# Attention values as seven block products, interleaved with the first query and key tiles

## The chip, the cores and the metric

The kernel runs on one core of one Trainium2 chip. The metric is the device time of one execution in microseconds. The core has a matrix engine (PE), a vector engine (DVE), an activation engine (ACT), a general engine (POOL), and SP, which here only issues DMAs. Each engine executes its own list of instructions in the order in which the program lists them; an instruction waits until the semaphores it names have reached a count, and everything behind it on the same engine waits with it.

## The reference, cut to what matters

Two layers on 512 tokens of 1024 features. Layer 0 mixes tokens with a gated linear recurrence, layer 1 with stick-breaking attention of 16 heads; after each mixer comes a SwiGLU feed-forward block (FFN), and every sub-layer is preceded by an RMS norm. The change touches layer 1 between its input and its first heads:

```
h   = rmsnorm(x, g)                       # 512 x 1024
qkv = h @ w_qkv                           # q, k, v: 512 x 1024 each, 16 heads of 64
z   = q k^T / 8;  w = exp(log_sigmoid(z) + suffix sums of log_sigmoid(-z)), masked
o   = w v                                 # per head
```

The sum `h @ w_v` is what is computed differently: a 512x1024 by 1024x1024 product.

## The kernel before, in words

Activations are kept transposed: `x[k]` holds features 128k to 128k+127 of all 512 tokens, 128 x 512. Everything is float32, and each product of two float32 numbers is made from three passes of the matrix engine: each factor is split into a high part (rounded to a shorter format, names ending in h) and a low part (the remainder, ending in l), and high times high, high times low and low times high are added in an accumulator bank (`bank`, eight of them, 128 x 512 each). So a weight chunk of 128 x 1024 goes through one DMA into a buffer (`raw`, `bu` or `bv`), one cast on ACT (`wh`) and one subtraction (`wl`) on DVE or POOL. `wh` and `wl` have three buffers each. The list `chunks` fixes in which order weight chunks are loaded, split and used; `chunk()` takes the next one and issues the splits and loads that lie a set number of chunks ahead.

The FFNs already use seven block products instead of eight: tokens are halved, features are halved, sums of quarters of the activations are formed on DVE and split by ACT and DVE, sums of quarters of the weights are formed by DMAs that add into their destination (`Piece.plus`, issued on POOL's queue), and the halves of the outputs are added up afterwards. `Piece` and `Unit` describe this.

In layer 1 the order around the change is this. At the end of the first FFN the last products are added to `x` (`take(m)`, DVE), and `gain(m)` makes the operands `uh` (ACT, x times the norm's gain) and `ul` (DVE) and the squares for the norm (ACT, summed in `acc` by POOL; the last one by DVE). `back(h)` transposes the FFN's output on PE. Between `back(0)` and `back(1)` stands the first of the value chunks. After it come, for two halves of the value columns, the products of all eight k with the four token tiles, 24 matmuls per chunk, eight chunks; between them the norm's statistics (`norm_rs1`: four small matmuls, a square root on ACT and a Newton step on DVE; `norm_rs2`: four transposing matmuls and a copy). The two halves are scaled and split into `vs` (ACT and DVE, `L1124` and `L1125`). Then come the query and key tiles (`proj(t)`, 24 matmuls, in two parts of 12; even t are queries, odd t keys), the first scores (`s1(0)`), the chain on them (`chain_a(0)`: nine activations on ACT, six DVE instructions, three on POOL), and `rsum`. From there a loop over heads takes scores, suffix sums (`s2`) and weighted values (`s3`) in turn, one more `proj` tile beside each head.

In the FFNs and from the first `proj` on, PE, ACT, DVE and POOL run in the order in which the code issues instructions. Between them, in the setup of the attention stage and in the value products, a scheduler orders them.

Of the kernel before, what the change touches and what calls it, by code (L numbers as in the profile page):

```python
# [10 lines left out]
F32 = mybir.dt.float32  # L11
F32R = mybir.dt.float32r
# [158 lines left out]
class Kern:  # L171
# [155 lines left out]
    def chunk(self, ahead=None):  # L327
# [9 lines left out]
        more = 11 if ffn else self.AHEAD_LOAD  # L337
# [201 lines left out]

        return gather, half, root, chain, store  # L540

    def v_chunk(self, pv, c):
        wh, wl = self.chunk()
        for kk in range(2):
            k = 2 * c + kk
            cs = ts(kk, S)
            for t in range(NT):
                uh, ul = self.u[k]
                self.mm3(pv[t], uh[:, ts(t)], ul[:, ts(t)], wh[:, cs], wl[:, cs], k == 0, k == KT - 1)

    def rglru(self):
        nc, tc = self.nc, self.tc
# [182 lines left out]
    def ffn(self, l, gnext):  # L735
# [3 lines left out]
        with tc.tile_pool(name=f"ffn{l}", bufs=1) as self.fp, \  # L739
# [2 lines left out]
            self.ffn_end = self.after[l] or len(self.chunks)  # L742
            self.hold = len(self.chunks)
            for i in range(self.used + 1, len(self.chunks)):
                if isinstance(self.chunks[i], Piece) and not isinstance(self.chunks[i - 1], Piece):
# [258 lines left out]
            if gnext:  # L1004
# [68 lines left out]
    def attention(self):  # L1073
# [5 lines left out]
        with ExitStack() as cx:  # L1079
# [28 lines left out]
                self.mi += 1  # L1108
                return mb[self.mi % len(mb)]

            for half in range(2):
                pv = [self.bank[4 - 4 * half + t] for t in range(NT)]
                for c in range(1 - half, 4):
                    self.v_chunk(pv, c)
                if half == 0:
                    self.bi = 2
                    self.norm_rs1()
                for t in range(NT):
                    r = self.rsT[:, t:t + 1]
                    pvv = pv[t].rearrange("p (h d) -> p h d", d=64)  # L1120
                    for j in range(2):
                        v = vs[t][2 * half + j] = self.new("vs", F32R, shape=[P, 4, P])
                        pj = pvv[:, 4 * j:4 * j + 4, :]
                        nc.scalar.activation(v[:, :, 0:64], pj, AF.Copy, scale=r)  # L1124
                        nc.vector.scalar_tensor_tensor(v[:, :, 64:128], pj, r, v[:, :, 0:64].bitcast(F32),  # L1125
                                                       ALU.mult, ALU.subtract)
                if half == 0:
                    self.bi = 3
                    self.norm_rs2()
            tc.keep_in_program_order(nc.scalar.preload_act_table_set("natural_log_exp_and_others"))  # L1130

            heads = {}
            self.qrel = []

            def proj(t, part):
                if part == 0:
                    self.pt = mps()
# [142 lines left out]
            E = mybir.EngineType  # L1280
            with tc.manual_schedule(engines={E.PE, E.Activation, E.DVE, E.Pool}):
                self.wl_dve = True
                for t in range(3):
                    proj(t, 0)
                    if t == 2:
                        s1(0)
                        chain_a(0)
                        for i in range(3):
                            rsum(0, i)
                    proj(t, 1)  # L1290
                    proj_evac1(t)
                    proj_evac2(t)
                self.wl_dve = False
                def osplit(p):
                    oh, ol = ou[p] = self.new("oh", F32R, True), self.new("ol", F32R, True)
# [116 lines left out]
def layout(inp):  # L1412
# [18 lines left out]
    v = wv.reshape(4, 2, P, 2, S).transpose(3, 0, 2, 1, 4).reshape(8, P, 1024)  # L1431
# [48 lines left out]
```

## Time and profile before

| | |
|---|---|
| median of 3 runs | 1103.15 us (1102.72 to 1103.34) |
| the profiled execution's own time | 1102.71 us |
| span of its trace | 1101.0 us |
| mean granted clock of PE | 0.998 |
| PE busy | 1087.4 us, 99% |
| DVE, ACT, POOL busy | 896.4, 710.8, 363.5 us |
| DMA | 159.87 MB, mean 145 GB/s |

The trace counts microseconds from the span's start. A row of its timeline gives start, duration, engine, line and operation with the tiles that it writes and reads. The duration of a matmul includes the passage through the array; consecutive matmuls overlap, and their rate is read from the distance of their starts. The value products run from 492.4 to about 539.8, the first query tiles from there, the first scores at 553.43, those of the second head at 560.42.

### The profile page before, as it was taken

To read this page: it belongs to the slowest core of one execution; us is meant where nothing else is said; L and a number is where in the kernel's file an instruction comes from. 1 tells how busy PE (TensorE), PEld (TensorE's weight loads), DVE (VectorE), ACT (ScalarE), POOL (GpSimd) and SP (SyncE) were. 2 spreads that over 40 slices of the span, in tenths; PEclk is the share of its full clock that TensorE was granted. 3 is DMA by queue.
4 is the path that set the end of the run, shared out by engine and by line. 5 is a ranking of instruction groups with operands and counts; after the bars stand their busy time and mean duration, and the time that the engine had idled before them with its cause. 6 is when DMAs were issued, how large, how long until landed. Compare 5 with 4: busy or idle time off the path is not lost.

```text
span 1101.0 us, 14735 instructions
## 1 busy us (share of the span) xinstructions
PE 1087.4 (99%) x5255; PEld 907.8 (82%) x5255; DVE 896.4 (81%) x1250; ACT 710.8 (65%) x1084; POOL 363.5 (33%) x273
## 2 busy tenths in 40 slices
PE   9999999999999999999999999999999999999996
PEld 6888888888888888888888888788888888888885
DVE  6967787687978888986378889978578797978897
ACT  6697667565546464635379999967764555546454
POOL 1652332324151413204034445413132424151412
PEclk9999999999999999999999999999999999999999
DMA  8532339877677776443243433234986777765522
GB/s 298 147 97 91 115 113 217 193 215 163 163 192 155 202 166 174 90 140 96 76 116 100 127 80 96 60 100 135 216 179 207 157 198 164 163 194 119 149 67 76
DMA packets 47385, 159.87 MB, mean 145 GB/s; under 512 B 5712, under 2 KB 5968, under 8 KB 47312
## 3 DMA queue, kind: packets, MB, share of 16 engines
q1 hardware_dynamic: 34640, 113.32, 31.8%
q0 software_dynamic: 12384, 45.09, 23.5%
q8 instruction: 41, 0.67, 0.3%
q10 hardware_dynamic: 288, 0.52, 0.1%
q14 instruction: 32, 0.26, 0.1%
HBM read 148.43 MB, written 2.10 MB: 137 GB/s over the span
## 4 chain that ended last, share of the span: by engine, by line
PE 75%; DVE 9%; ACT 4%; issue 3%; DVEq 0%
PE bank L771 17%; PE bank L772 17%; PE bank L773 17%; PE bank L350 6%; PE bank L352 6%; PE bank L351 6%; DVE wl L315 3%; PE bank L1238 2%; DVE y L763 1%; PE bank L778 1%; PE bank L1264 1%; ACT t L1202 1%; ACT t L1201 1%; ACT wh L313 1%; DVE ks L1167 1%
## 5 line engine op out<-in xcount | busy, mean ns | idle before, releaser
L315 DVE TENSOR_TENSOR wl<-raw,wh 128x1024 fp32r<-128x1024 f32 x114 | 171.6, 1507 | 39.9 <-ACT wh L313 39.5
L313 ACT CAST wh<-raw 128x1024 fp32r<-128x1024 f32 x134 | 140.1, 1048 | 94.9 <-PE bank L773 37.2
L771 PE MATMUL bank<-wh,ow 128*128 128x512 f32 (+1 forms) x480 | 179.6, 374 | 0.5 <-DVE b L763 0.5
L773 PE MATMUL bank<-wh,ow 128*128 128x512 f32 (+1 forms) x480 | 178.3, 372 | 0.0
L772 PE MATMUL bank<-wl,ow 128*128 128x512 f32 (+1 forms) x480 | 178.3, 371 | 0.0
L92 POOL DMA_DIRECT2D bu<-w_gu x64 | 56.1, 877 | 277.3 <-DMA bu<-w_gu 159.1
L313 ACT CAST wh<-bu 128x1024 fp32r<-128x1024 f32 x66 | 69.5, 1053 | 65.1 <-PE bank L773 39.8
L315 DVE TENSOR_TENSOR wl<-bu,wh 128x1024 fp32r<-128x1024 f32 x66 | 82.9, 1273 | 28.9 <-ACT wh L313 28.1
L771 PEld LDWEIGHTS bank<-wh,ow 128*128 128x128 f32 x480 | 90.4, 188 | 16.7 <-issue 1.3
L773 PEld LDWEIGHTS bank<-wh,ow 128*128 128x128 f32 x480 | 90.4, 188 | 15.7
L772 PEld LDWEIGHTS bank<-wl,ow 128*128 128x128 f32 x480 | 90.5, 188 | 15.4
L350 PE MATMUL bank<-uh,wh 128*128 128x512 f32 x256 | 101.5, 398 | 1.4 <-ACT wh L656 1.4
L351 PE MATMUL bank<-ul,wh 128*128 128x512 f32 x256 | 99.6, 390 | 0.0
L352 PE MATMUL bank<-uh,wl 128*128 128x512 f32 x256 | 99.5, 391 | 0.0
L763 DVE TENSOR_TENSOR y<-y,bank 128x512 f32<-128x512 f32 x140 | 89.0, 679 | 2.2 <-PE bank L773 2.1
L315 POOL TENSOR_TENSOR wl<-raw,wh 128x1024 fp32r<-128x1024 f32 x22 | 55.8, 2540 | 80.1 <-ACT wh L313 68.4
L771 PE MATMUL bank<-wh,hth 128*128 128x512 f32 (+1 forms) x194 | 75.4, 389 | 0.0
L772 PE MATMUL bank<-wl,hth 128*128 128x512 f32 (+1 forms) x194 | 75.3, 388 | 0.0
L773 PE MATMUL bank<-wh,htl 128*128 128x512 f32 (+1 forms) x194 | 75.1, 387 | 0.0
L315 DVE TENSOR_TENSOR wl<-bv,wh 128x1024 fp32r<-128x1024 f32 x44 | 58.3, 1337 | 13.3 <-ACT wh L313 13.2
L1206 POOL TENSOR_TENSOR spl<-t,sph 128x512 fp32r<-128x512 f32 (+1 forms) x32 | 38.9, 1235 | 82.9 <-DVE sph L1205 80.7
L350 PEld LDWEIGHTS bank<-uh,wh 128*128 128x128 f32 x256 | 48.0, 188 | 11.5 <-ACT wh L656 2.5
(277 smaller groups left out, 2770.3 us busy)
## 6 DMA issues: line engine op xcount, KB each, us to landing
bu<-w_gu POOLq DMA_DIRECT2D x64, 512.0 KB, 5.8
raw<-w_gu SPq DMA_DIRECT2D x44, 512.0 KB, 4.1
raw<-w_dn SPq DMA_DIRECT2D x24, 512.0 KB, 5.4
bu<-w_gu SPq DMA_DIRECT2D x22, 512.0 KB, 4.3
bv<-w_gu SPq DMA_DIRECT2D x22, 512.0 KB, 4.1
bv<-w_gu POOLq DMA_DIRECT2D x22, 512.0 KB, 6.4
d<-w_dn SPq DMA_DIRECT2D x20, 512.0 KB, 3.7
raw<-w_qk SPq DMA_DIRECT2D x16, 512.0 KB, 3.6
```

Source lines behind the costliest of these rows:

```text
L92: kern.soon(lambda: kern.nc.gpsimd.dma_start(t, self.part(n), accum_op=ALU.add))
L313: (self.nc.vector.tensor_copy if self.wh_dve else self.nc.scalar.copy)(wh[:, c], raw)
L315: self.wli = self.wl_engine(i).tensor_tensor(wl[:, c], raw, wh[:, c].bitcast(F32), ALU.subtract)
L350: mm(out, lhsT=wh, rhs=xh, start=first, stop=False)
L351: mm(out, lhsT=wh, rhs=xl, start=False, stop=False)
L352: mm(out, lhsT=wl, rhs=xh, start=False, stop=last)
L763: add = lambda o, a, b: nc.vector.tensor_tensor(o, a, b, ALU.add)
L771: mm(out, lhsT=xh, rhs=wh, start=first, stop=False, skip_group_check=True)
L772: mm(out, lhsT=xh, rhs=wl, start=False, stop=False, skip_group_check=True)
L773: mm(out, lhsT=xl, rhs=wh, start=False, stop=last, skip_group_check=True)
L1206: nc.gpsimd.tensor_tensor(sl[:, w], sp[:, w], sh[:, w].bitcast(F32), ALU.subtract)
L1238: mm(zt[kt][:, o0:o0 + ZW[j]], lhsT=tri if j == kt else one_n, rhs=s_, start=False, stop=True, skip_group_check=True)
```

## The change

The value product is cut into two halves of tokens (columns 0 to 255 and 256 to 511 of the transposed activations, `lo` and `hi`), two halves of features (k 0 to 3 and 4 to 7) and two halves of value columns. It is made from seven block products instead of eight, numbered 1 to 7. Each has two weight chunks of 12 matmuls. `VUnit` gives them, and the three query and key chunks between them, their order: product 1, query/key tiles 0, 1, 2, products 5, 3, 6, 2, 7, 4. Eight accumulating DMAs of 512 KB, two to a sum, make the weight sums in the buffers `bu` and `bv`: `bu` gets a second quarter for product 5, a third for 6 and a fourth for 4; `bv` gets a second quarter for 7. Those for product 5 are issued ahead of the stage. The prefetch of the second FFN's first chunks into the same two buffers moves behind the value products.

The activation sums are formed in two steps for each k of 0 to 3: `vops1(k)` makes two scaled copies of x (ACT), a difference and a second difference of 128 x 256 (DVE), and splits the result (`vh` by ACT, `vl` by DVE); `vops2(k)` makes two more sums of 128 x 256 and splits them. Products 5 and 6 need `vops1`, 3 and 7 need `vops2`; 1, 2 and 4 use the plain `uh` and `ul`.

Three bank pairs are used: A (4, 5), B (2, 3) and B2 (0, 1). Product 1 is written to A and copied to `r1`; 5 to B and copied to `b5`; 3 is added on top of B, 6 on top of A; A is copied to `u2`, to which B is added; 2 goes to B2 and is added to `r1`; 7 on top of A, added to `b5`; 4 on top of A. Each finished half is scaled and split into `vs` (`v_evac`). `norm_rs1`, `norm_rs2` and `vops2` stand around product 5, the evacuations of tiles 0 to 2 around product 3. `s1(0)`, `chain_a(0)` and `rsum` now stand ahead of product 4, and the third query/key tile is no longer split around them. The loop over heads is unchanged.

On ACT, from the norm's table load on. `vs` are the values, `acc` receives the norm's broadcast, `wh` are weight casts. Before:

```order
L469 ACT_TABLE_LOAD
L469 ACTIVATE x_79<-bank_72,eps 128x4
L1124 ACTIVATE vs_4349<-bank_74,x_79 128x4x64
L1124 ACTIVATE vs_4355<-bank_75,x_79 128x4x64
L1124 ACTIVATE vs_4361<-bank_76,x_79 128x4x64
L1124 ACTIVATE vs_4367<-bank_77,x_79 128x4x64
L1124 ACTIVATE vs_4352<-bank_74,x_79 128x4x64
L1124 ACTIVATE vs_4358<-bank_75,x_79 128x4x64
L491 COPY acc<-bank_73 128x512
L1124 ACTIVATE vs_4364<-bank_76,x_79 128x4x64
L1124 ACTIVATE vs_4370<-bank_77,x_79 128x4x64
L313 CAST wh_4434<-raw_4013 128x1024
```

And now, where `vh` are the activation sums, `vb` the copy of product 5 out of banks 2 and 3:

```order
L486 ACT_TABLE_LOAD
L486 ACTIVATE x_79<-bank_71,eps 128x4
L1346 ACT_TABLE_LOAD
L1298 CAST vh_4420<-vw_4285 128x512
L1298 CAST vh_4426<-vw_4314 128x512
L329 CAST wh_4431<-bv_4015 128x1024
L508 COPY acc<-bank_71 128x512
L1298 CAST vh_4454<-vw_4368 128x512
L1298 CAST vh_4460<-vw_4379 128x512
L329 CAST wh_4465<-bv_4035 128x1024
L1294 COPY vb_4264<-bank_72 128x512
L1294 COPY vb_4265<-bank_73 128x512
```

Where the value evacuations followed the square root, there now stand four casts of activation sums, the copy of the norm, and two weight casts ahead of the copies out of banks 2 and 3.

On DVE at the same place, right behind the norm's statistics (`vw` are the sums being formed, `vl` their low parts, `wl_4432` is the low part of product 3's first chunk):

```order
L1313 SCALAR_TENSOR_TENSOR vw_4285<-vw_4285,vw_4286 128x256
L1287 TENSOR_TENSOR vw_4285<-vw_4284 128x256
L1287 TENSOR_TENSOR vl_4421<-vw_4285,vh_4420 128x512
L1313 SCALAR_TENSOR_TENSOR vw_4314<-vw_4314,vw_4315 128x256
L1287 TENSOR_TENSOR vw_4314<-vw_4313 128x256
L1287 TENSOR_TENSOR vl_4427<-vw_4314,vh_4426 128x512
L331 TENSOR_TENSOR wl_4432<-bv_4015,wh_4431 128x1024
L1313 SCALAR_TENSOR_TENSOR vw_4368<-vw_4368,vw_4369 128x256
L1287 TENSOR_TENSOR vw_4368<-vw_4367 128x256
L1287 TENSOR_TENSOR vl_4455<-vw_4368,vh_4454 128x512
L1313 SCALAR_TENSOR_TENSOR vw_4379<-vw_4379,vw_4380 128x256
L1287 TENSOR_TENSOR vw_4379<-vw_4378 128x256
```

Before, DVE had eight evacuations of values and two weight subtractions here; now it has four times two sums and a low part, with one weight subtraction between the second and the third.

On ACT around the first head's chain (its nine `t` activations). Before:

```order
L313 CAST wh_4607<-raw_4468 128x1024
L1201 ACTIVATE t_4636<-bank_70 128x512
L1202 ACTIVATE t_4636<-t_4636 128x512
L1203 ACTIVATE t_4636<-t_4636 128x512
L1201 ACTIVATE t_4646<-bank_71 128x384
L1202 ACTIVATE t_4646<-t_4646 128x384
L1203 ACTIVATE t_4646<-t_4646 128x384
L1201 ACTIVATE t_4656<-bank_72 128x384
L1202 ACTIVATE t_4656<-t_4656 128x384
L1203 ACTIVATE t_4656<-t_4656 128x384
L1153 CAST qx_4684<-t_4682 128x512
L313 CAST wh_4700<-raw_4525 128x1024
```

And now, from the chain's last two activations on:

```order
L1204 ACTIVATE t_4745<-t_4745 128x384
L1205 ACTIVATE t_4745<-t_4745 128x384
L329 CAST wh_4759<-raw_4566 128x1024
L329 CAST wh_4777<-raw_4584 128x1024
L1325 ACTIVATE vs_4795<-bank_74,x_79 128x4x64
L1325 ACTIVATE vs_4798<-bank_74,x_79 128x4x64
```

Before, the cast for the key tile 3 (`wh_4607`) stood ahead of the chain; now that cast (`wh_4759`) and the one for tile 4 stand behind it, and the values of product 4 behind them. On DVE the corresponding subtraction (`wl_4760`) stands behind `rsum` in the same way.

The diff, without the layout of the list of chunks' loads and the unchanged bodies:

```diff
+V_POOL = (8, 10, 12, 14, 16)
+class VUnit:
+    np, kt, u, direct = 2, 2, -1, False
+    def __init__(self, kern):
+        self.kern, self.src, self.b = kern, kern.a["w_v"], {}
+        self.order = (1, "k", "k", "k", 5, 3, 6, 2, 7, 4)
...
-        full += [a["w_v"][c] for c in range(8)]
-        full += [a["w_qk"][t] for t in range(16)]
+        for q in self.vu.order:
+            full += [qk.pop(0)] if q == "k" else [Piece(self.vu, q, c) for c in range(2)]
...
+        self.wl_on.update({self.v0 + j: self.nc.gpsimd if j in V_POOL else self.nc.vector
+                           for j in range(self.v1 - self.v0)})
...
-        ahead = ahead or (4 if ffn else self.AHEAD_SPLIT)
+        ahead = ahead or (4 if ffn else 3 if v else self.AHEAD_SPLIT)
...
-                self.v_chunk(self.bank[4:], 0)
+                self.vprod(1, self.bank[4:6], 0)
                 gain(2, 3)
                 back(1)
+                self.vprod(1, self.bank[4:6], 1)
...
+                def vops1(k):
+                    ua, ub, w1 = w[k] = [self.new("vw") for _ in range(3)]
+                    nc.scalar.activation(ua, self.x[k], AF.Copy, scale=self.col("g_mix1", k))
+                    nc.scalar.activation(ub, self.x[k + 4], AF.Copy, scale=self.col("g_mix1", k + 4))
+                    sub(w1[:, lo], ub[:, hi], ua[:, hi])
+                    nc.vector.scalar_tensor_tensor(w1[:, hi], w1[:, lo], -1.0, ua[:, lo], ALU.mult, ALU.subtract)
+                    h, l = vsplit(w1)
...
+                def vops2(k):
+                    ua, ub, w1 = w[k]
+                    nc.vector.scalar_tensor_tensor(ub[:, hi], ub[:, lo], -1.0, w1[:, hi], ALU.mult, ALU.subtract)
+                    sub(ub[:, lo], ua[:, lo], ua[:, hi])
+                    h, l = vsplit(ub)
...
+                copies(r1, A)
+                for t in range(2):
+                    proj(t, 0)
+                    vops1(t)
+                for t in range(2):
+                    proj(t, 1)
+                proj(2, 0, self.bank[0])
+                vops1(2)
+                vops1(3)
+                proj(2, 1)
+                self.norm_rs1()
+                vops2(0)
+                vops2(1)
+                self.vprod(5, B, 0)
+                self.norm_rs2()
+                vops2(2)
+                vops2(3)
+                self.vprod(5, B, 1)
+                copies(b5, B)
+                proj_out(0)
+                for c in range(2):
+                    self.vprod(3, B, c, False)
+                    proj_out(1 + c)
...
+                s1(0)
+                chain_a(0)
+                for i in range(3):
+                    rsum(0, i)
+                for c in range(2):
+                    self.vprod(4, A, c, False)
+                for t in range(2):
+                    v_evac(2 + t, 0, A[t])
```

More of the change, by code (lines that the diff above doesn't have):

```diff
@@ L250, in plan @@
         self.after = [len(full), None]
-        full += [a["w_v"][c] for c in range(8)]
-        full += [a["w_qk"][t] for t in range(16)]
+        self.vu = VUnit(self)
+        self.v0 = len(full)
+        qk = [a["w_qk"][t] for t in range(16)]
+        for q in self.vu.order:
+            full += [qk.pop(0)] if q == "k" else [Piece(self.vu, q, c) for c in range(2)]
+        self.v1 = len(full)
+        full += qk
+        self.wl_on.update({self.v0 + j: self.nc.gpsimd if j in V_POOL else self.nc.vector
+                           for j in range(self.v1 - self.v0)})
         full += [a["w_bo"][m] for m in range(8)]
@@ L540, in final, with vprod @@
         return gather, half, root, chain, store
-    def v_chunk(self, pv, c):
+    def vprod(self, q, out, c, first=True):
+        mm = self.nc.tensor.matmul
         wh, wl = self.chunk()
[L544 to L549, printed above, removed]
+        lo = slice(0, HS) if q in (1, 2) else slice(HS, S)
+        for j in range(2):
+            for i in range(2):
+                k = 2 * c + i
+                oh, ol = (t[:, lo] for t in self.u[k + (0 if q == 1 else 4)]) if q in (1, 2, 4) else self.vops[k][q]
+                h, l = wh[:, ts(i, S)], wl[:, ts(i, S)]
+                mm(out[j], lhsT=oh[:, ts(j)], rhs=h, start=first and k == 0, stop=False, skip_group_check=True)
+                mm(out[j], lhsT=oh[:, ts(j)], rhs=l, start=False, stop=False, skip_group_check=True)
+                mm(out[j], lhsT=ol[:, ts(j)], rhs=h, start=False, stop=k == 3, skip_group_check=True)
     def rglru(self):
@@ L744, in ffn @@
             for i in range(self.used + 1, len(self.chunks)):
-                if isinstance(self.chunks[i], Piece) and not isinstance(self.chunks[i - 1], Piece):
+                if isinstance(self.chunks[i], Piece) and not isinstance(self.chunks[i - 1], Piece) and not \
+                        self.v0 <= i < self.v1:
                     self.hold = i + 8
@@ L1109, in mps, with proj @@
                 return mb[self.mi % len(mb)]
[L1111 to L1130, printed above, removed]
             heads = {}
             self.qrel = []
-            def proj(t, part):
+            def proj(t, part, bank=None):
                 if part == 0:
-                    self.pt = mps()
+                    self.pt = bank or mps()
                     self.pw = self.chunk()
@@ L1282, in attention @@
                 self.wl_dve = True
-                for t in range(3):
-                    proj(t, 0)
[L1285 to L1289, printed above, removed]
-                    proj(t, 1)
+                A, B, B2 = self.bank[4:6], self.bank[2:4], self.bank[0:2]
+                lo, hi = slice(0, HS), slice(HS, S)
+                sub = lambda o, x, y: nc.vector.tensor_tensor(o, x, y, ALU.subtract)
@@ new lines, in attention, with copies, vsplit @@
+                add = lambda o, x, y: nc.vector.tensor_tensor(o, x, y, ALU.add)
+                r1, u2, b5 = ([self.new(n) for _ in range(2)] for n in ("vr", "vu", "vb"))
+                self.vops, w = [None] * 4, [None] * 4
+                def copies(dst, src):
+                    for x, y in zip(dst, src):
+                        nc.scalar.copy(x, y)
+                def vsplit(src):
+                    h, l = self.new("vh", F32R), self.new("vl", F32R)
+                    nc.scalar.copy(h, src)
+                    sub(l, src, h.bitcast(F32))
+                    return h, l
@@ new lines, in vops1 @@
+                def vops1(k):
[5 more added lines that the diff above has]
+                    h, l = vsplit(w1)
+                    self.vops[k] = {5: (h[:, lo], l[:, lo]), 6: (h[:, hi], l[:, hi]), 1: (h, l)}
@@ new lines, in vops2, with v_evac @@
+                def vops2(k):
[3 more added lines that the diff above has]
+                    h, l = vsplit(ub)
+                    self.rel(ua, ub, w1)
+                    self.vops[k].update({7: (h[:, lo], l[:, lo]), 3: (h[:, hi], l[:, hi]), 0: (h, l)})
+                def v_evac(t, half, src):
+                    r = (self.nrs if half else self.rsT)[:, t:t + 1]
+                    pvv = src.rearrange("p (h d) -> p h d", d=64)
+                    for j in range(2):
+                        v = vs[t][2 * half + j] = self.new("vs", F32R, shape=[P, 4, P])
+                        pj = pvv[:, 4 * j:4 * j + 4, :]
+                        nc.scalar.activation(v[:, :, 0:64], pj, AF.Copy, scale=r)
+                        nc.vector.scalar_tensor_tensor(v[:, :, 64:128], pj, r, v[:, :, 0:64].bitcast(F32),
+                                                       ALU.mult, ALU.subtract)
@@ L1291, in attention @@
                     proj_evac1(t)
                     proj_evac2(t)
+                proj_out(0)
[3 more added lines that the diff above has]
+                for c in range(2):
+                    self.vprod(6, A, c, False)
+                self.rel(*(t for e in self.vops for t in e[1]))
+                copies(u2, A)
+                for x, y in zip(u2, B):
+                    add(x, x, y)
+                for t in range(2):
+                    v_evac(t, 1, u2[t])
@@ new lines, in attention @@
+                self.rel(*u2)
+                for c in range(2):
+                    self.vprod(2, B2, c)
+                for x, y in zip(r1, B2):
+                    add(x, x, y)
+                for t in range(2):
+                    v_evac(t, 0, r1[t])
+                self.rel(*r1)
+                for c in range(2):
+                    self.vprod(7, A, c, False)
+                self.rel(*(t for e in self.vops for t in e[0]))
+                for x, y in zip(b5, A):
+                    add(x, x, y)
@@ L1293, in attention @@
+                for t in range(2):
+                    v_evac(2 + t, 1, b5[t])
+                self.rel(*b5)
+                s1(0)
+                chain_a(0)
+                for i in range(3):
+                    rsum(0, i)
+                for c in range(2):
+                    self.vprod(4, A, c, False)
+                for t in range(2):
+                    v_evac(2 + t, 0, A[t])
                 self.wl_dve = False
```

15 lines of the change are left out of this document (13 added, 2 removed).

## The prediction

> **What bounds the kernel now.** I read the page's shares first, then busy time by stretch over the place of the change, then the timelines of each engine there.
>
> ```profile
> PE 1087.4 (99%) x5255; PEld 907.8 (82%) x5255; DVE 896.4 (81%) x1250; ACT 710.8 (65%) x1084; POOL 363.5 (33%) x273
> PE   9999999999999999999999999999999999999996
> core 0: us, PE busy (x) PEld busy (x) DVE busy (x) ACT busy (x) POOL busy (x), PEclk, DMA share, GB/s
> 492.00:511.00 19.00, 19.00 (x93) 15.66 (x92) 15.57 (x19) 11.45 (x18) 11.54 (x8) 1.00 0.18 56
> 511.00:545.00 34.00, 34.00 (x159) 28.44 (x158) 12.68 (x31) 14.93 (x25) 5.07 (x3) 1.00 0.30 93
> 545.00:561.00 16.00, 16.00 (x77) 13.03 (x77) 10.07 (x15) 8.59 (x14) 3.07 (x3) 1.00 0.50 131
> ```
>
> PE is busy in all of the page's 40 slices and never idle here. But DVE is at 82% from 492 to 511, and only the value products behind that, where DVE is at 37% and ACT at 44%, leave room. So PE bounds the stage by the slack that plain value products give the other engines, and the question is what becomes of that slack.
>
> A matmul costs the distance between starts:
>
> ```profile
> 492.40 0.39 PE L350 MATMUL bank<-wh,uh 128*128 128x512 f32 x1
> 492.63 0.39 PE L351 MATMUL bank<-wl,uh 128*128 128x512 f32 x1
> 492.86 0.39 PE L352 MATMUL bank<-wh,ul 128*128 128x512 f32 x1
> 493.08 0.39 PE L350 MATMUL bank<-wh,uh 128*128 128x512 f32 x1
> ```
>
> That is 0.227 us. The change removes 192 - 168 = 24 of them: **-5.4 us**, if PE stays fed. The rest of this text is about whether it does.
>
> **The new work.** Splitting goes from 8 value chunks of 24 matmuls to 14 of 12: one chunk each 2.7 us. New beside it are eight activation sums. Their pieces have these rows (in order: a weight cast and subtraction, differences of 256 columns, a cast and low part of 512, a copy out of a bank, and a scaled copy of x):
>
> ```profile
> 510.96 1.05 ACT L313 CAST wh<-raw 128x1024 fp32r<-128x1024 f32 x1 [1.25 <-PE bank L352]
> 554.00 1.23 DVE L315 TENSOR_TENSOR wl<-raw,wh 128x1024 fp32r<-128x1024 f32 x1 [0.31 <-ACT wh L313]
> 560.04 0.42 DVE L1214 TENSOR_TENSOR t<-sp 128x256 f32<-128x256 f32 x1
> 562.57 0.62 ACT L1153 CAST qx<-t 128x512 fp32r<-128x512 f32 x1 [3.50 <-DVE t L1145]
> 563.22 0.69 DVE L1154 TENSOR_TENSOR qy<-t,qx 128x512 fp32r<-128x512 f32 x1 [0.69 <-ACT qx L1153]
> 522.13 0.62 ACT L491 COPY acc<-bank 128x512 f32<-128x512 f32 x1
> 504.17 0.73 ACT L408 ACTIVATE uh<-x,x 128x512 fp32r<-128x512 f32 x1 [2.80 <-DVE x L763]
> ```
>
> One sum is a round trip, and DVE and ACT take their instructions in order, so nothing behind it fills the wait: 0.42 + 0.42 with about 0.03 per handover (562.57 + 0.62 to 563.22), 0.62 on ACT, and 0.60 until DVE can start the next (starts follow one another some 0.08 sooner than the durations say, as 0.68 at 507.74 does below). That makes 2.16 us. The existing operands show the same pattern at the same price, take, `uh`, `ul`, take:
>
> ```profile
> 499.40 0.68 DVE L763 TENSOR_TENSOR x<-x,bank 128x512 f32<-128x512 f32 x1
> 500.87 2.66 DVE L409 SCALAR_TENSOR_TENSOR ul<-x,x,uh 128x512 fp32r<-128x512 f32 x1 [0.61 <-ACT uh L408]
> 503.45 0.68 DVE L763 TENSOR_TENSOR x<-x,bank 128x512 f32<-128x512 f32 x1
> 505.60 0.68 DVE L763 TENSOR_TENSOR x<-x,bank 128x512 f32<-128x512 f32 x1
> 507.74 0.68 DVE L763 TENSOR_TENSOR x<-x,bank 128x512 f32<-128x512 f32 x1
> 508.54 1.55 DVE L315 TENSOR_TENSOR wl<-raw,wh 128x1024 fp32r<-128x1024 f32 x1
> 510.00 0.74 DVE L409 SCALAR_TENSOR_TENSOR ul<-x,x,uh 128x512 fp32r<-128x512 f32 x1
> 500.59 2.39 POOL L315 TENSOR_TENSOR wl<-raw,wh 128x1024 fp32r<-128x1024 f32 x1
> ```
>
> 2.15 and 2.14 us. The last row explains the 2.66: an elementwise DVE instruction on two SBUF tiles stands while POOL runs one.
>
> **Step A, the last `ul`.** It ended at 510.74. With 12 instead of 24 matmuls ahead of `back(1)` its chain could start 2.7 us sooner, but DVE must first finish two `ul` and a third chunk's `wl` that now precede it, and one more `wl` and `vops1(0)` stand inside it; POOL's `wl` leaves it. Laid out with the rows above, take of x[4] falls at 501.7 and the last `ul` ends at **511.7**. Bounds: 508.0 (all of the 2.7 gained) and 513.6 (one more wait on POOL like that in the 2.66, 1.9 over the 0.74 of its neighbour).
>
> **Step B, from there to the release of banks 2 and 3.** Product 3 adds onto product 5 in these banks, so it waits for ACT's copies to `b5`, and these stand on ACT behind all four `vops2` casts and a weight cast. The chain is this. The weight cast of 5's first chunk waits for its buffer until tile 0 is done, two matmuls after 511.7; it ends its slot at 513.15, 0.1 short of its end as on DVE. `vops1(1)`: two scaled copies (0.63 + 0.73), two DVE steps (0.95 with handovers), cast 0.62: 516.05. The second weight cast and `vops1(2)`: 519.8. `vops1(3)`, 2.8: 522.6. Then the norm, with these rows:
>
> ```profile
> 517.51 1.28 ACT L469 ACT_TABLE_LOAD   x1
> 518.81 0.26 ACT L469 ACTIVATE x<-bank,eps 128x4 f32<-128x4 f32 x1
> 519.10 0.16 DVE L470 TENSOR_SCALAR x<-bank 128x4 f32<-128x4 f32 x1 [0.35 <-ACT x L469]
> 520.77 2.44 DVE L1125 SCALAR_TENSOR_TENSOR vs<-bank,x,vs 128x256 fp32r<-128x256 f32 x6
> ```
>
> The table load stands behind the cast: 524.1 after the root. DVE's steps, 519.10 to 520.77 and a small negation: 525.9. `vops2(0)` and `vops2(1)`, 2.16 each: 530.2. The `wl` of product 3 waits for its cast behind the second `vh`: 531.75. `vops2(2)`: 533.9. `vops2(3)` up to the end of its cast: 535.45. The cast of 3's second chunk, then the first copy, 0.95 + 0.62: **product 3 starts at 537.0**.
>
> PE by itself would be there long before: after 511.7 it has 38 matmuls of the three tiles (to 520.3), 12 of product 5, the norm's transposes, which wait for 525.9, and 12 more, 529.5 in all. So it idles 2 to 3 us for the transposes and, in one piece, 7 to 8 us for the banks. Lower bound for B: if the ACT and DVE halves of the eight sums overlapped, 0.62 less for each of the seven on the path, 4.3 sooner.
>
> **Step C, the clock.** The trace of before has no such idle time except at its start:
>
> ```profile
> 1.26 3.77 PE L387 MATMUL bank<-warm 128*128 128x512 bf16 x9 [1.26 <-DVE warm L385]
> ```
>
> Nine matmuls took 3.77, 0.42 each against 0.227 later; out of rest PE loses 9 x 0.19 = 1.7 us. I take 1.7 for the long idle piece; bounds 0 and 1.7. [...]
>
> **Step D, to the second head's scores.** After 537.0 + 1.7: products 3, 6, 2, 7 are 96 matmuls, 21.8; `s1(0)` and product 4 (24, 5.4) follow. The first scores' rows, and the chain on them:
>
> ```profile
> 553.43 0.39 PE L1181 MATMUL bank<-qh,ks 128*128 128x512 f32 x1
> 554.86 0.48 PE L350 MATMUL bank<-uh,wh 128*128 128x512 f32 x1
> 558.54 0.53 ACT L1203 ACTIVATE t<-t 128x384 f32<-128x384 f32 x1
> 561.50 0.42 DVE L1219 TENSOR_TENSOR r<-t,r 128x256 fp32r<-128x256 f32 x1
> 560.42 0.39 PE L1181 MATMUL bank<-qh,ks 128*128 128x512 f32 x1
> ```
>
> `s1(0)` takes 1.43, so it ends at 562.0 and key tile 3 could start at 567.4. But its weight cast stands on ACT behind the chain, which ends 4.2 us after the scores (559.07 - 554.86), and its `wl` on DVE behind `rsum`, 7.05 us after (561.92 - 554.86): 569.0, and 570.2 with 1.23. PE needs it at 567.85 and waits 2.35. (Bounds: 0, and 4.25 with another wait of 1.9 on POOL, whose three subtractions of the chain run just then: the cast at 560.49 below takes 0.98 for 256 columns.) Tile 3's first half ends at 572.5, and the second head's scores start there, against 560.42 before: **+12.1 us**. In both kernels only half a tile lies between; all that follows is unchanged. That the first head's chain now has product 4 as cover buys little, as before it had 24 matmuls of tiles as cover too.
>
> ```profile
> 560.49 0.98 DVE L1217 CAST r<-t 128x256 fp32r<-128x256 f32 x1
> 572.98 0.50 PE L1181 MATMUL bank<-qh,ks 128*128 128x512 f32 x1 [0.35 <-DVE awl L1253]
> ```
>
> The stall of the third head (0.35 and a few tenths behind it) can go or stay; I leave it. 1102.71 + 12.1 = 1114.8 for the profiled execution, 0.44 under the median: I forecast **1115 us**.
>
> **What I cost at nothing.** The accumulating DMAs: they land 5.8 us after issue by the page's row below. The sum for 6 is issued once 5's `wl` is made, near 514 and 518, and used after 537; those for 7 and 4 have at least four chunks, 10.9 us, between. Without that cover each late one would cost up to 5.8. POOL has the five `wl` of 2.39 with 2.7 us per chunk, and queues an accumulating issue behind one only where the sum is far from use. The moved prefetch of the second FFN has some 200 us.
>
> ```profile
> bu<-w_gu POOLq DMA_DIRECT2D x64, 512.0 KB, 5.8
> ```
>
> **The rivals.** First, **PE stays fed**: the round trips of `vops2` fit under products and the 24 matmuls are gained, with perhaps 0.4 of the third head's stall: 1102.71 - 5.4 - 0.4 = 1097. For it: the FFNs run the same density of chunks with PE full (the row of slices above). Against it: their sums are made from the layer's tail before the products, and here ACT has four of them between product 5 and the copy that product 3 needs. It decides if product 3 starts by 523.6 (the 31.4 us of PE work of step D ahead of 555.0, which is 560.42 - 5.4). Second, **half of it**: the last `ul` at 508, sums overlapping (-4.3), no clock loss, tile 3 not waiting. 12.1 - 3.7 - 4.3 - 1.7 - 2.35 = 0: 1103. With about half of these, 1108. For it: each bound is possible; against: three independent ones must go the same way, and the 2.15 pattern is in the trace. Third, **a late weight sum on top**: POOL does an accumulating issue and a `wl` in order; if a `wl` waits long for its cast, the issue behind it starts late, and product 6 or 7 waits 5.8 for it: 1115 + 5.8 = 1121. Against: the slack of at least 10.9.
>
> **How the numbers follow.** Forecast near 1115 (1110 to 1119): 0.65. Half of it, 1103 to 1110: 0.20, of which 0.05 within 0.2% (2.2 us, what a measurement of this kernel can tell from no change). PE stays fed: 0.07. Late sum: 0.08. Range 1105 to 1119: the lower end takes in most of the second case, the upper POOL's collisions (+1.9 in A and in D) on top of the sum. Faster by over 0.2%: 0.08; within: 0.05; slower: 0.87.
>
> **What would show it.** In the changed profile: one idle piece of PE of 7 to 8 us ahead of the first matmul of product 3, its releaser the ACT copy of `vb`; one of 2 to 3 ahead of the norm's transposes; about 2.4 at tile 3, released by DVE's `wl`; the granted clock at half behind the longest. I am wrong if PE shows no idle time over 2 us between the last `ul` and product 3, or if the second head's scores start before 562.

## The result and the profile after

The changed kernel takes 1119.05 us (median of four runs, 1118.28 to 1120.09) against 1103.18 for the kernel before beside it: 1.0145 times as long, 95% interval 1.0128 to 1.0163. The forecast was 1115 with a range of 1105 to 1119. The direction and most of the path were right; the time is 4 us above the forecast and just outside the range. The profile below is of the slowest of the four executions, 1120.09 us.

The page of the changed kernel, its first lines on busy time and the slices of PE and of its granted clock:

```profile
PE 1088.2 (97%) x5231; PEld 905.7 (81%) x5231; DVE 922.2 (82%) x1285; ACT 729.6 (65%) x1112; POOL 375.3 (34%) x283
PE   9999999999999999998889999999999999999997
PEclk9999999999999999999889999999999999999999
```

There are 24 matmuls less, and yet PE is busy for 0.8 us longer: some run at half clock. DVE has 25.8 us more work, ACT 18.8. The damage is in three slices, which busy time by stretch resolves (the same stretches as in the prediction, and one more):

```profile
492.00:511.00 19.00, 16.91 (x76) 12.18 (x76) 17.48 (x23) 14.21 (x22) 9.32 (x7) 1.00 0.26 83
511.00:545.00 34.00, 24.90 (x107) 20.04 (x108) 23.33 (x45) 21.38 (x30) 8.95 (x8) 0.90 0.47 80
545.00:561.00 16.00, 16.00 (x73) 13.09 (x72) 12.06 (x18) 10.82 (x18) 8.34 (x5) 1.00 0.96 250
561.00:583.00 22.00, 17.25 (x73) 13.48 (x73) 15.16 (x25) 13.39 (x26) 6.45 (x7) 0.84 0.59 173
```

What PE waited for between 485 and 620 (instruction waiting, what ended the wait, us in total, times, longest):

```profile
PE bank L568 <- ACT vb L1294: 7.8, 1, 7.8
PE bank L369 <- DVE wl L331: 4.3, 1, 4.3
PE bank L507 <- DVE t L493: 1.3, 1, 1.3
PE bank L570 <- DVE ul L426: 0.7, 1, 0.7
PE bank L367 <- ACT uh L425: 0.6, 1, 0.6
PE bank L368 <- DVE ul L426: 0.5, 1, 0.5
PE bank L367 <- ACT wh L329: 0.5, 1, 0.5
```

In order of time: the last splits of the normalized rows (0.7, 0.6, 0.5), the norm's transposes (1.3), product 3 (7.8), key tile 3 (0.5 and 4.3). An eighth, 0.2 at the third head, is left out here; the kernel before has it too. The PE rows at the two long ones, and the start of the second head's scores:

```profile
536.45 0.79 PE L568 MATMUL bank<-wh,vh 128*128 128x512 f32 x1 [7.83 <-ACT vb L1294]
537.04 0.63 PE L569 MATMUL bank<-wl,vh 128*128 128x512 f32 x1
...
540.79 0.39 PE L569 MATMUL bank<-wl,vh 128*128 128x512 f32 x1
...
572.95 0.80 PE L369 MATMUL bank<-uh,wl 128*128 128x512 f32 x1 [4.28 <-DVE wl L331]
573.54 0.63 PE L367 MATMUL bank<-uh,wh 128*128 128x512 f32 x1
...
577.38 0.63 PE L1183 MATMUL bank<-qh,ks 128*128 128x512 f32 x1
```

From 537.04 nine matmuls take 3.75 us, and from 573.54 nine take 3.84: about 0.42 each in place of 0.227, and the granted clock is 0.54 from 537 to 541. The second head's scores start 17.0 us later than before (560.42), and the span is 17.4 longer (1118.4 to 1101.0): all of the loss arises here. Between starts of matmuls the seven waits come to 17.0 (each row counts 0.1 to 0.2 less, from the end that the trace gives for the matmul ahead) and the half clock up to there to 4.2; with -5.4 for the matmuls saved that leaves 1.2 for smaller pieces. The other 0.4 of the span is half clock in the second head's first two matmuls.

Why key tile 3 waited so long is seen on POOL, DVE and ACT:

```profile
565.38 0.89 POOL L101 DMA_DIRECT2D bu<-w_gu  x1 [4.01 <-DVE sph L1207]
566.59 0.89 POOL L101 DMA_DIRECT2D bu<-w_gu  x1 [0.32 <-issue]
567.15 2.58 POOL L1208 TENSOR_TENSOR spl<-t,sph 128x512 fp32r<-128x512 f32 x2
567.92 3.05 DVE L1216 TENSOR_TENSOR t<-sp 128x256 f32<-128x256 f32 x1
...
571.67 2.35 DVE L331 TENSOR_TENSOR wl<-raw,wh 128x1024 fp32r<-128x1024 f32 x2
566.85 1.98 ACT L329 CAST wh<-raw 128x1024 fp32r<-128x1024 f32 x2
```

Two issues of the second FFN's accumulating prefetch stand on POOL ahead of the first head's `spl`. So the `spl` run when DVE has come to `rsum`, whose first step takes 3.05 us beside them in place of 0.42, and tile 3's `wl` follows `rsum`. (The first row names DVE's `sph` as what ended the issue's wait; experiment 2 shows that it was another.) Its cast on ACT was done by 568: DVE is what it waited for.

### The profile page after: what moved, and what is told of

Its sections match the earlier page's. It is cut to its first block, busy times and chain, and to the rows that moved or that the text cites. A ratio compares the mean times of both kernels' runs of the same rounds, so it can differ in the third digit from the quotient of the medians.

```text
span 1118.4 us, 14779 instructions
## 1 busy us (share of the span) xinstructions
PE 1088.2 (97%) x5231; PEld 905.7 (81%) x5231; DVE 922.2 (82%) x1285; ACT 729.6 (65%) x1112; POOL 375.3 (34%) x283
## 4 chain that ended last, share of the span: by engine, by line
PE 67%; DVE 13%; ACT 6%; issue 4%; DMA 2%; DVEq 0%; POOL 0%; POOLq 0%; ACTq 0%
PE bank L793 15%; PE bank L794 15%; PE bank L795 15%; PE bank L369 5%; PE bank L367 5%; PE bank L368 5%; DVE wl L331 4%; PE bank L1240 2%; DMA bu<-w_gu 2%; DVE y L785 2%; PE bank L1266 1%; ACT wh L329 1%; PE bank L800 1%; PE bank L568 1%; ACT t L1204 1%
## 5 line engine op out<-in xcount | busy, mean ns | idle before, releaser
L329 ACT CAST wh<-raw 128x1024 fp32r<-128x1024 f32 x130 | 135.8, 1048 | 79.5 <-PE bank L795 34.5
L331 DVE TENSOR_TENSOR wl<-raw,wh 128x1024 fp32r<-128x1024 f32 x112 | 168.7, 1509 | 21.9 <-ACT wh L329 21.8
L329 ACT CAST wh<-bu 128x1024 fp32r<-128x1024 f32 x72 | 75.7, 1052 | 64.2 <-PE bank L795 38.3
L331 DVE TENSOR_TENSOR wl<-bu,wh 128x1024 fp32r<-128x1024 f32 x70 | 86.9, 1258 | 29.7 <-ACT wh L329 28.9
L331 DVE TENSOR_TENSOR wl<-bv,wh 128x1024 fp32r<-128x1024 f32 x46 | 60.6, 1327 | 17.3 <-ACT wh L329 17.2
L331 POOL TENSOR_TENSOR wl<-raw,wh 128x1024 fp32r<-128x1024 f32 x20 | 50.8, 2543 | 69.6 <-ACT wh L329 57.9
L329 ACT CAST wh<-bv 128x1024 fp32r<-128x1024 f32 x48 | 49.7, 1048 | 22.4 <-PE bank L795 13.5
L369 PEld LDWEIGHTS bank<-uh,wl 128*128 128x128 f32 x256 | 48.6, 190 | 15.1 <-DVE wl L331 4.7
```

The costliest lines, as they stand in the source:

```text
L329: (self.nc.vector.tensor_copy if self.wh_dve else self.nc.scalar.copy)(wh[:, c], raw)
L331: self.wli = self.wl_engine(i).tensor_tensor(wl[:, c], raw, wh[:, c].bitcast(F32), ALU.subtract)
L369: mm(out, lhsT=wl, rhs=xh, start=False, stop=last)
```

## The experiments

All are edits of the changed kernel, and each ratio is to the kernel before, run beside it. The cuts of their code are shortened, with some lines in words. "Less than the change" is against its median of 1119.05; the median of the kernel before lay between 1102.57 and 1103.18 in the different batches, so differences of some 0.6 us say nothing.

**1 (e1). POOL's queue at tile 3.** The two issues go behind the last `spl` of head 0:

```
-  kern.soon(lambda: kern.nc.gpsimd.dma_start(t, self.part(n), accum_op=ALU.add))
+  def add():                       # mark: head 0's last spl, for the FFN's first unit alone
+      with kern.tc.issue_after(mark.ins) if mark else ExitStack():
+          kern.nc.gpsimd.dma_start(t, self.part(n), accum_op=ALU.add)
+  kern.soon(add)
```

> The change as it is, except that the two accumulating DMAs of the second FFN's first unit are issued on POOL behind head 0's three spl and not ahead of them. Theory P (POOL's queue set the wait at key tile 3: the two issues stand there 4.01 and 0.89 us, the spl run late, and rsum's first step lasts 3.05 us beside them): rsum's first step is back near the 0.42 us of before, the wait for wl ahead of tile 3 falls from 4.3 us to about 2.3, and if the idle stretch of 0.6 + 2.3 us is short enough for the clock to stay up, another 2 us of half clock go; 1115 to 1117 us. Rival Q (the wait is set by ACT's exps and the weight cast behind them, whatever POOL does): the wait stays above 4 us and the time within 1 us of 1119.

1116.37 us, ratio 1.0123 (1.0109 to 1.0137): 2.7 less than the change. DVE and POOL at the place:

```profile
568.70 0.41 DVE L1224 TENSOR_TENSOR t<-sp 128x256 f32<-128x256 f32 x1
569.92 1.81 POOL L104 DMA_DIRECT2D bu<-w_gu  x2
```

The step is back at 0.41 and the wait between starts fell from 4.45 to 2.49. P holds and Q falls. Half clock still followed (7 matmuls, 1.4 us; the granted clock is 0.92 from 561 to 583), which P had left open.

**2 (e2). Tile 3's split ahead of head 0's chain.**

```
                 self.rel(*b5)
+                self.split_one()
                 s1(0)
```

> The change as it is, except that key tile 3's weight cast on ACT and its wl on DVE stand ahead of head 0's scores, exps and rsum. Both P and Q: tile 3 no longer waits, so the 4.3 us ahead of its third matmul and the 2 us of half clock behind it go; about 1112 to 1113 us. Rival R (the time is set by head 0's chain, so that what is taken from tile 3 comes back as a wait in the scores of head 1 or in head 0's values): the idle time turns up again ahead of the scores of head 1 or of a later step and the time stays at 1118 to 1119.

1118.26, ratio 1.0141 (1.0127 to 1.0155), not told apart from the change. The wait moved, as R said; PE's only wait from 555 to 585:

```profile
PE bank L1183 <- DVE vs L1326: 4.8, 2, 4.4
```

and POOL and DVE in that time:

```profile
566.18 0.89 POOL L101 DMA_DIRECT2D bu<-w_gu  x1 [4.70 <-DMA bu<-w_gu]
568.97 2.87 DVE L1216 TENSOR_TENSOR t<-sp 128x256 f32<-128x256 f32 x1
...
572.55 1.22 DVE L331 TENSOR_TENSOR wl<-raw,wh 128x1024 fp32r<-128x1024 f32 x1
```

Head 1's scores need banks 4 and 5, and these hold product 4 until DVE has evacuated it, behind the same 2.87 us step and the next `wl`. So R's mechanism was near, but not the one named: not the chain itself, but the evacuation queued behind it. The first of these rows shows what the issue on POOL waits for: the landing of the load onto which it adds. The `sph` that the change's row names cannot be it, as here the issue starts at 566.18 and that `sph` ends at 566.3.

**3 (e5). Both, and the evacuation ahead of `rsum`.**

```
                 chain_a(0)
-                for i in range(3):
-                    rsum(0, i)
                 ... product 4 and its evacuation
+                for i in range(3):
+                    rsum(0, i)
```

> The change as it is with three edits around head 0: the accumulating DMAs of the second FFN behind head 0's spl on POOL (as in e1), tile 3's cast and wl ahead of head 0's exps (as in e2), and product 4's evacuation ahead of rsum on DVE. Theory P2 (in e2 the wait only moved: head 1's scores waited 4.4 us for DVE's evacuation of product 4, which stood behind rsum's 2.87 us step and a wl of 1.22): the evacuation is about 4 us sooner, head 1's scores wait 1 us or less, no half clock follows, and from the scores of head 0 to those of head 1 it takes about 10.7 us in place of 17.07; 1112 to 1114 us. Rival R2 (head 1's scores wait for head 0's chain itself, whose exps cannot be sooner): 3 us or more of wait stay there; 1116 or more.

1113.95, ratio 1.0098 (1.0085 to 1.0112): 5.1 less than the change.

```profile
PE bank L1189 <- DVE vs L1334: 1.7, 2, 0.9
```

From the first head's scores to the second's it is 9.7 us in place of 17.1, and no half clock falls in it: the first scores (1.43) and 36 matmuls at 0.227 make 9.6. Two waits of 0.9 stand inside the second head's scores. P2 holds.

**4 (e3). Extra matmuls in the hole ahead of product 3.**

```
+                for _ in range(24):
+                    mm(self.bank[1], lhsT=self.u[0][0][:, ts(0)], rhs=self.u[0][0], start=True, stop=True)
                 copies(b5, B)
```

> The change as it is, with 24 extra 512-column matmuls whose result nothing uses (about 24 x 0.227 = 5.4 us) between product 5 and product 3, where PE idles 7.99 us. Theory C (the nine matmuls at 0.427 us behind that hole are the clock's answer to the idle time): product 3 starts at the same 536.6, its matmuls come every 0.227 us from the first on, and 1.8 us are saved: 1117.2. Rival D (product 3 is slow for another reason: operands arriving one by one, or a port that ACT and DVE load): the nine stay near 0.43 us and the time stays at 1119.

1118.34, ratio 1.0140 (1.0126 to 1.0155), not told apart from the change. The 24 matmuls had to wait for bank 1, which ACT's copy of the norm releases. Their row and the first of product 3:

```profile
532.05 7.36 PE L1356 MATMUL bank<-uh 128*128 128x512 f32 x24 [1.89 <-ACT acc L508]
539.25 0.39 PE L568 MATMUL bank<-wh,vh 128*128 128x512 f32 x1
```

Busy time by stretch (the last three columns are the granted clock, the DMA share and GB/s):

```profile
526.00:532.00 6.00, 3.92 (x20) 3.07 (x20) 4.20 (x12) 2.96 (x5) 0.00 (x0) 1.00 0.00 0
532.00:534.00 2.00, 1.95 (x8) 1.59 (x9) 1.54 (x3) 0.34 (x1) 0.86 (x1) 0.88 0.00 0
534.00:537.00 3.00, 3.00 (x9) 2.32 (x8) 1.92 (x4) 1.39 (x3) 0.00 (x0) 0.51 0.81 134
```

Product 3 runs at full clock from its first matmul (0.23 between starts, granted clock 1.00 from 537 to 540): the slow matmuls are the clock's, and D falls. But the half clock came all the same, inside the extra matmuls, though no idle piece here was longer than 2.05 us. So filling bought nothing: product 3 came 1.3 us later behind product 5 (9.5 between starts, 8.2 in the change), which took back most of the 2 us that it gained in clock.

**5 (e4). Product 6 in the hole.**

```
-        self.order = (1, "k", "k", "k", 5, 3, 6, 2, 7, 4)
+        self.order = (1, "k", "k", "k", 5, 6, 3, 2, 7, 4)
```

with the products in that order in the code.

> The change with the block products in the order 1, 5, 6, 3, 2, 7, 4: product 6, whose operands are ready before the second set of sums, stands in the hole ahead of product 3. Theory H (product 3 is late since ACT's copies of product 5 stand behind the second set's casts; nothing else is near): 24 matmuls (5.4 us) fill most of the 7.99 us, the half clock behind it goes (1.8 us), about 2.5 us of wait stay ahead of product 3; 1111 to 1113. Rival W (product 6's weights, summed by an accumulating DMA on product 5's, are not there by 529): product 6 waits in its turn, and the hole only moves; 1117 to 1120.

1120.34, ratio 1.0157 (1.0143 to 1.0172): no gain. The three largest waits between 520 and 560:

```profile
PE bank L569 <- POOL wl L331: 1.9, 1, 1.9
PE bank L568 <- ACT wh L329: 1.7, 2, 1.4
PE bank L569 <- DVE wl L331: 1.5, 2, 0.8
```

ACT's rows there:

```profile
529.43 1.04 ACT L329 CAST wh<-bu 128x1024 fp32r<-128x1024 f32 x1
...
534.84 0.62 ACT L1298 CAST vh<-vw 128x512 fp32r<-128x512 f32 x1 [1.60 <-DVE vw L1287]
535.36 1.04 ACT L329 CAST wh<-bu 128x1024 fp32r<-128x1024 f32 x1
```

The activations of product 6 were ready, its weights were not: their casts stand on ACT behind the second set's casts too (529.43 behind the second, 535.36 behind the fourth). H's "nothing else is near" is wrong; W is right that the hole moves, not in its cause: both casts start without a wait as soon as ACT's queue comes to them, so the summed weights were there.

**6 (e9). No weight sums.** The eight accumulating DMAs of the value weights are left out (`plus` does nothing for the value unit), so the values of attention are other numbers.

> The change without the eight accumulating DMAs on the value weights: each block product gets its plain weight block, so the values of attention are other numbers; every matmul, cast and rest stays. Theory N (the accumulating DMAs land long before their casts, and the waits are made by ACT's and DVE's queues): no hole changes by more than 0.5 us; 1118 to 1120. Rival S (a late weight sum, or POOL standing at the issue of one, holds product 3 or a later product): 2 us or more are saved; 1117 or less.

1119.40, ratio 1.0147 (1.0133 to 1.0161 against 1.0128 to 1.0163 with them): no difference. In its trace the hole is 8.0 and tile 3's wait 4.36. N holds: the weight sums of the value product cost nothing that these runs can tell.

**7 (e6). No second set.** `vops2` hands out the first set's operands, so the values are other numbers here too.

```
-                    nc.vector.scalar_tensor_tensor(ub[:, hi], ...)      # two sums
-                    sub(ub[:, lo], ua[:, lo], ua[:, hi])
-                    h, l = vsplit(ub)                                   # cast and rest
+                    h, l = self.vops[k][1]
```

> The change without the sums, casts and rests of the second set of operands: products 3 and 7 use the first set's operands, so the values of attention are other numbers; the matmuls and DMAs stay the same in count and shape. Theory H2 (the 7.99 us hole ahead of product 3 is the time of the four sums-cast-rest chains of 2.23 us and of what is queued behind them on ACT): product 3 starts within 1 us of the end of product 5, the half clock behind the hole goes too; 8 to 10 us are saved: 1109 to 1111. Rival W2 (product 3's weights, or their sums by DMA, are as late as that): the hole keeps most of its length; 1116 or more.

1111.79, ratio 1.0076 (1.0063 to 1.0088): 7.3 less, somewhat under the 8 to 10 expected. Its largest waits from 515 to 575:

```profile
PE bank L369 <- DVE wl L331: 5.0, 1, 5.0
PE bank L507 <- DVE t L493: 1.3, 1, 1.3
PE bank L569 <- POOL wl L331: 0.9, 1, 0.9
```

The hole and its half clock are gone (matmuls start 0.22 to 0.23 apart from 527.79 to 530.05); 0.7 came back at tile 3 and 0.9 at a `wl` on POOL. H2 holds.

**8 (e7). The second set written out in another order**, nothing left out (the order in words):

```
-  vops2(0); vops2(1); product 5, first half; norm_rs2; vops2(2); vops2(3); product 5, second half; copies(b5, B)
+  sums(0) ahead of norm_rs1; cast(0); sums(1); cast(1); rest(0); sums(2); rest(1); product 5; copies(b5, B)
+  norm_rs2; cast(2); sums(3); cast(3); weight split of product 3's second half; rest(2); rest(3)
```

> The change with the second set written out in another order: the four chains of sums, cast and rest overlap (sums of the next k ahead of the rest of this one), the first sums stand ahead of the norm, ACT's copies of product 5 stand ahead of the casts for k 2 and 3, and the transposes of the norm stand behind product 5. Theory L (each chain of 2.23 us is mostly handover: DVE 0.42 + 0.42 + 0.69, ACT 0.62, each waiting for the other, so that order alone shortens it): product 3 starts near 531.5 with 2 to 3 us of idle time in pieces, its second half waits 2 us for a wl on POOL, the 1.43 us at the transposes goes, half clock is little; 1112 to 1114. Rival B (DVE and ACT are busy with work that has to be done there anyway): 1 to 2 us saved at most; 1117 to 1118.

1114.02 (1110.21 to 1115.03), ratio 1.0102 (1.0087 to 1.0118): 5.0 less. Its waits from 520 to 540:

```profile
PE bank L570 <- POOL wl L332: 1.9, 1, 1.9
PE bank L569 <- ACT vb L1295: 1.2, 1, 1.2
PE bank L570 <- DVE wl L332: 0.5, 1, 0.5
```

In place of 7.8 and 1.3 there are 1.2, 0.5 and 1.9, with the same instructions on ACT and DVE: L holds, B falls. The edit does more than overlap the chains: ACT's copies of product 5 stand ahead of two casts, and the transposes behind product 5. What each of these is worth alone was not run. (The executions spread more than others, and the profiled one was the fastest; in it tile 3's `wl` was late by 1.6 and not 4.3, so the saving is read from the median.) Half clock followed product 3's pieces still (7 matmuls), behind idle pieces of 1.4, 0.77 and 2.05 between starts; the granted clock is 0.53 from 535 to 538.

**9 (e8, e10). Together.** The edits of e5 and e7, with the first set overlapped in the same way (e8), and then with the second half of tile 3 ahead of head 1's scores and the first `wl` of product 6 on POOL in place of the second (e10):

```
-                        if h == 1:        # second half of the tile ahead of the scores
+                        if h < 2:
-V_POOL = (8, 10, 12, 14, 16)
+V_POOL = (8, 9, 12, 14, 16)
```

> The edits of e5 and e7 together, and the first set's chains overlapped in the same way. If their savings add (about 6 and 6, and 1 for the first set): 1105 to 1107, which is still above the kernel before. If the stall only moves down the line to the next queue: 1111 or more. If the first set was what held up the projections too: 1103 or less.

> The kernel of e8 with the second half of key tile 3's projection ahead of head 1's scores (12 matmuls, 2.7 us, where they waited 2.0), and product 6's first weight rest on POOL, its second on DVE. If the 2.0 us of wait there is covered: 1106 to 1107.5. If it comes back behind the scores of head 1, as a wait in head 0's weights: 1108 or more. A time under 1103, that of the kernel before, would need 3 us more than any wait that is left there.

e8: 1108.15, ratio 1.0053 (1.0041 to 1.0066), 1 us above what was expected. e10: 1107.30, ratio 1.0038 (1.0024 to 1.0052), as expected, though not told apart from e8. Of the 15.9 us lost, 11 to 12 came from the order of work on three queues and could be had back by order alone. What is left in e8 is short waits for the copies of product 5 (2.3), `wl` on POOL (2.0), `vs` (1.7) and splits. e10 took away the wait for `vs` and part of that for POOL, and 0.9 us at most came of it; other cures were not run. No version run here with the whole computation beats the kernel before.

**10 (e11, e12). Without the operands' sums.** Both sets left out: products 5, 6, 3, 7 read `uh` and `ul` (e11), which gives other numbers; then with the edits at tile 3 as well (e12).

```
                 def vops1(k):
+                    h, l = self.u[k]
+                    self.vops[k] = {5: (h[:, lo], l[:, lo]), 6: (h[:, hi], l[:, hi])}
```

and likewise `vops2` for products 3 and 7.

> The change without both sets of operands: products 5, 6, 3 and 7 read the splits of the normalized rows that are there anyway, so the values of attention are other numbers; the matmuls and DMAs stay the same in count and shape. Theory A (the sums, casts and rests of the operands on ACT and DVE are what the change costs between 505 and 545): the hole of 7.99 us, its 1.8 us of half clock and the 1.43 us at the transposes go, and what is left are the three short waits for the last splits and the stall at tile 3; 1106 to 1108. Rival E (the queues of ACT and DVE are as full there with casts and rests of the weights): 1111 or more.

> e11 with the edits at head 0 and tile 3 of e5 and e10. Theory A: the 24 matmuls less (5.4 us) show at last, less the waits for the last splits (2 to 3 us): 1100 to 1101.5, faster than the kernel before. Rival E: 1105 or more. If it comes to 1103 to 1104.5, a part of the loss belongs to neither the operands nor tile 3.

e11: 1108.05, ratio 1.0049 (1.0035 to 1.0062). e12: 1100.09, ratio 0.9974 (0.9964 to 0.9985), faster than the kernel before by 2.8. Busy time by stretch of e12:

```profile
511.00:545.00 34.00, 33.54 (x156) 27.65 (x155) 20.01 (x35) 20.77 (x29) 15.26 (x11) 1.00 0.73 143
561.00:583.00 22.00, 21.29 (x116) 17.30 (x115) 19.88 (x34) 20.36 (x39) 10.10 (x8) 1.00 0.41 97
```

PE is full and its clock whole. Theory A holds in both. The account from the change: 11.0 us for the operands' sums and 8.0 for head 0 and tile 3, and the 2.8 that remain of the saving are the 5.4 less the three waits for the last splits (2.2 between starts) and one of 0.6 for a `wl`. (11.0 + 8.0 - 2.8 is 16.2 and not 15.9, as the kernel before was 0.3 faster in this batch.)

## Why the prediction was right and wrong

**24 matmuls, -5.4: right** as far as the account of e12 goes: 2.8 us gained, and the rest in four short waits.

**Step A (last `ul` at 511.7): right.** It ended 0.9 sooner:

```profile
510.06 0.74 DVE L426 SCALAR_TENSOR_TENSOR ul<-x,x,uh 128x512 fp32r<-128x512 f32 x1
```

**Step B (product 3 at 537.0, 7 to 8 us idle in one piece, released by the copy of `vb`): right.** 536.45, 7.83 us, that releaser. The end of the chain reads as laid out, the fourth cast, a weight cast, the copies:

```profile
534.35 0.62 ACT L1298 CAST vh<-vw 128x512 fp32r<-128x512 f32 x1 [1.61 <-DVE vw L1287]
534.87 1.04 ACT L329 CAST wh<-bv 128x1024 fp32r<-128x1024 f32 x1
535.82 1.06 ACT L1294 COPY vb<-bank 128x512 f32<-128x512 f32 x2
```

e6 and e7 confirm the cause from both sides: without the second set the hole is gone, and with the same work in another order most of it is. Only the wait at the transposes was sized too large (2 to 3; 1.3): they start at 524.70 behind the first of DVE's four steps `t`, and the forecast had them wait for all four and the negation.

**Step C (1.7 us of half clock behind the long idle piece): right in size, in part by luck, and counted once.** Nine matmuls took 3.75 where 2.04 is usual, 1.7. But the nine of the forecast were all the warm-up matmuls that the kernel issues at its start, not the length of a slow stretch, and the granted clock of before reads 1.00 over them (0 to 4 us). Behind the same idle piece five ran at 0.42 to 0.43 us in e2 and e9, eight here and eleven in e5, and the granted clock from 511 to 545 was 0.90 here and 0.85 in e1. The same question was not asked of tile 3's wait, and there it cost more: ten matmuls from 572.95 to the second head's scores at 577.38 take 4.43 in place of 2.27.

**Step D is where it failed.** The wait at tile 3 was put at 2.35, and its bound, 4.25, was the measured row (4.28). Step D named what would lead to the bound, POOL's three subtractions running beside DVE, but gave no reason why they should not. What makes them run just then was passed over in "What I cost at nothing": "The moved prefetch of the second FFN has some 200 us." That asked when the prefetched weights are needed. It did not ask who stands behind their issue on POOL: the first head's `spl`, which then collided with `rsum`. e1 measures that sentence at 2.7 us; without the collision the wait is 2.49, near the 2.35 of the sum. The other part, which the sum put at nothing, is the half clock behind the same wait. Of the 4.9 by which the second head's scores came later than forecast (577.4, not 572.5), 2.1 are the longer wait (4.45 between starts, not 2.35), 2.2 the clock and 0.5 the wait for the cast `wh` ahead of the tile.

Step D also took tile 3's split to be the only thing in the way. e2 shows a second one behind it: product 4's evacuation, queued on DVE behind `rsum`, holds the banks of the second head's scores. "That the first head's chain now has product 4 as cover" overlooked that this cover uses two of these banks.

**The rivals.** A late weight sum: no, and e9 shows no cost of the sums at all. PE stays fed and half of it: neither came; e12 at 1100 is what the first would have been worth here, 3 above its 1097, since the last splits still hold PE for 2.2.

**The range** added POOL's collisions at A and D to the sum and reached 1119; a second stretch of half clock was not in it. With its 2.2 the time would have been well inside.

## What to carry to other kernels

Price a moved DMA issue by what stands behind it on its queue, not by when its data is due: here two issues with 200 us to spare cost 2.7 us. Before trading matmuls for sums, write down each new operand's way through the engines as a chain of handovers; the four chains of 2.2 us of the second set held PE for 7.8 us, and another order of the same work gave back 5.0 of the 15.9 lost (e7). A wait that is removed is worth only what the next wait behind it allows (e2). And PE waits are to be charged with their half clock too: here it followed waits that came to 2.6 us within 3 us in e4 (1.57 and 1.03 between starts; the eight matmuls from 532.36 took 3.38 in place of 1.82) and to 2.4 in e7 (0.63 and 1.81).

## What the runs showed of the hardware

Half clock followed less idle time than the 7 to 8 us for which the forecast counted it. In e3 PE's idle pieces ahead of it were 1.42 and 2.05 us between starts, 5 us apart, in e7 1.4, 0.77 and 2.05 within 8 us; eight and seven matmuls at half rate followed, for 3.4 and 3.0 us. No half clock followed 1.49 alone in e8 (granted clock 1.00 from 545 to 561), its two waits of 0.9 for `vs` (1.00 from 561 to 583), or 1.06 and 0.97 together in e5. And it does not always start with the first matmul behind the wait: in e3 the extra matmuls ran at full rate from 532.05 to about 533.6 and only then at half (granted clock 0.51 from 534 to 537). In e12, whose waits are all under 1 us, the granted clock is 1.00 in all stretches here. The slow stretches lasted from 2.7 us (e8) to 5.6 us (e5). What sets their start and their length the runs do not show; idle pieces of about 2 us and less, with work between them, were enough.

What the prediction says of DVE beside POOL shows in the trace of before. DVE's `wl` from `raw`, on two SBUF tiles, took 1.23 us at most in the 80 rows with nothing on POOL but DMA issues, and 2.24 in the mean of the 27 that overlap a POOL instruction by more than 0.3 us (1.20 to 3.27). `sph` of 384 columns, which reads a bank, took 0.54 in the mean of 6 rows without POOL and 0.55 in the mean of 18 beside it.
